# A one layer hybrid trunk on one core: the masked pairs written by VectorE, the norm sums and spreads asked for later

## The chip, the core and the metric

The kernel runs on one core of one Trainium2 chip. The metric is the device time of one execution in microseconds, the median of several runs. The engines are called PE (TensorE, matrix products and transposes), DVE (VectorE), ACT (ScalarE), POOL (GpSimd) and SP (SyncE, which issues DMAs here); PSUM banks take the results of PE.

## What is computed

One decoder layer on 2048 tokens of width 1024, all in float32: an RMSNorm with a shift and a scale from a conditioning vector, one combined input projection, three kinds of causal token mixers side by side, a per-head norm, a swish gate and an output projection; then a second norm, a gated feed-forward part with a causal convolution of width 3, and a last norm. Chunks have 64 tokens.

```python
def reference(x, c, w_in, ...):
    for l in range(DEPTH):                                   # DEPTH = 1
        mod = (c_act @ w_ada[l] + b_ada[l])[:, None, :]
        sh1, sc1, g1, sh2, sc2, g2 = jnp.split(mod, 6, axis=-1)
        h = rms_norm(x) * (1.0 + sc1) + sh1
        x = x + g1 * token_mixer(h, ...)                     # retention | HGRN2 | GLA, one in- and one out-projection
        h = rms_norm(x) * (1.0 + sc2) + sh2
        x = x + g2 * conv_ffn(h, ...)
    return rms_norm(x) * final_gain

# HGRN2 (8 heads, dk 64) and GLA (4 heads, dk 32): per-channel decay, one step per chunk
    cum = jnp.cumsum(gn, axis=2)
    rel = jnp.where(causal, cum[:, :, :, None, :] - cum[:, :, None, :, :], -jnp.inf)
    attn = jnp.einsum('bhid,bhjd,bhijd->bhij', qn, kn, jnp.exp(rel))
    o = jnp.einsum('bhij,bhje->bhie', attn, vn) + jnp.einsum('bhid,bhde->bhie', qn * jnp.exp(cum), s)
```

Retention (4 heads) has a fixed decay for each head instead. The attention inside a chunk, `attn`, is what the moved instruction begins to write.

## The kernel before

**Blocks and units.** The tokens are cut into four blocks of 512. In each block seven mixer units run in the order h0, h1, g, h2, h3, r0, r1: an h unit holds two HGRN2 heads, the g unit all GLA heads in two halves ("subs"), an r unit two retention heads. Tile names carry that letter (`ath`, `atg`, `qbg`, `kg`). The feed-forward part runs afterwards in two super-blocks of 1024 tokens. Almost every product is three matmuls (lines L254 to L256, operands split in a high and a low part), 128x512 or 128x256 each.

**Attention in a chunk** is `gated()`. The products of q and k on the diagonal, and of neighbours in a pair, are made by DVE, turned by four transposes each (L639), and summed (L643) into `dot`. One instruction (L649) multiplies them, broadcast, by a mask of pairs and so writes the whole 128x1024 tile `ath` or `atg`: the diagonal, the first level, and zeros elsewhere. Six levels follow (2, 4, ... 64 tokens): PE makes the level's products (L662, tile `lvh` or `lvg`), DVE decays q and k for the next level (L670, L672) and copies the level's quarter into the tile (L681, predicated; the widest ones are copied by ACT at L678). A later level waits for the decays of the one before. Then come the turned keys (L687), the state's update (`u` L701, `S` L711) and the outputs (L594, L596). There are 24 multiplies of L649: four units of h and two halves of g in each of four blocks.

**Norms.** The sum of squares of a block over its columns is gathered in an accumulator (`san` for the first and second norm, `n3a` for the last): a load of x on SP's queue, a square on ACT (L358), an add on DVE (L359), eight times. `rstd()` then has two parts: `first()` turns the accumulator by four transposes (`ssn`, L337), sums it on DVE and makes the reciprocal root by Newton steps (L155, L158 to L160, `rsn`); `second()`, `gap` later, spreads it over the partitions by four transposes (`bcn`, L348) and a copy on ACT. The same Newton lines serve the per-head norms of the mixers (`omsh`, `orsh`).

**What sets the order.** PE's order is written by hand through a clock of estimated time, `Clock`: every product advances it, and `clock.at(us, fn)` puts `fn` on the list at `us` from now. It is called when its time is reached while the main stream of projections is being written, so a larger number puts an operation further down PE's queue. `gated()` is a generator in such a list; its `yield PAIR_GAP` and `yield LEVEL_GAP` are the estimated time until its next operations. The other engines' order comes from a scheduler with priorities (`tc.high_priority(offset=CHAIN)` brings the chain of a unit forward), so it shifts with PE's. All engines work off their queue in order.

**Other work around it.** `sgg` (L561) are DVE's adds of the gate projection's parts; they free PSUM banks which the next projection, `pshfh`, needs. `es` (L1093 to L1096) are DVE's edge operations on tiles loaded from a scratch buffer in DRAM (`h2d`), for the feed-forward part; `wsd` (L945 to L948) are the same kind for weights. L316 and L247 split weights for the three matmuls. L365 and the `n2` jobs use the spreads.

Of the kernel before, what the change touches and what calls it, by code (L numbers as in the profile page):

```python
# [23 lines left out]
NB = SEQ // TB  # L24
# [26 lines left out]
CHAIN = 400  # L51

M512, M256, MF = 0.227, 0.12, 0.224
LEVEL_GAP, PAIR_GAP = (3.2, 4.8), 4.4
POST_GAP, LAST_GAP = 16.0, 12.0
JOB_RATE = 1.8

# [47 lines left out]
def trunk(ctx, tc, xT, vecs, cvec, cst, rope, msk, wada, win, walow, wgla, wout, wup, wdown, out):  # L105
# [13 lines left out]
    clock = Clock()  # L119
# [13 lines left out]
    def tmp(name, shape=(P, 512)):  # L133
        return pt.tile(list(shape), F32, tag="te", name=name, bufs=NTE)
# [4 lines left out]
    def small(name, n=8):  # L139
        return pc.tile([P, n], F32, tag="sm", name=name, bufs=8)  # L140

    V, S, G, T = nc.vector, nc.scalar, nc.gpsimd, nc.tensor
# [10 lines left out]
    def newton(x, y, n):  # L153

        V.tensor_scalar(y[:].bitcast(I32), x[:].bitcast(I32), -0.5, MAGIC, op0=ALU.mult, op1=ALU.add)  # L155
        a = small("nw", n)
        for _ in range(3):
            V.scalar_tensor_tensor(a[:], y[:], -0.5, y[:], op0=ALU.mult, op1=ALU.mult)  # L158
            V.tensor_tensor(a[:], a[:], x[:], op=ALU.mult)  # L159
            V.scalar_tensor_tensor(y[:], a[:], 1.5, y[:], op0=ALU.add, op1=ALU.mult)  # L160
# [97 lines left out]
    h = [None] * KD  # L258
# [71 lines left out]
    def rstd(acc, name, bc, then, bank=None, gap=4.5):  # L330

        bank = bank or late_ps

        def first():
            p = bank("ss" + name)
            for c in range(NCH):
                T.transpose(p[:, c * P:(c + 1) * P], acc[:, c * P:(c + 1) * P], ident)  # L337
            x, r = small("ms" + name, NCH), small("rs" + name, NCH)
            with tc.high_priority(offset=CHAIN):
                V.tensor_reduce(x[:], p[:].rearrange("p (c d) -> p c d", c=NCH), axis=mybir.AxisListType.X, op=ALU.add)  # L340
                V.tensor_scalar(x[:], x[:], 1.0 / D, EPS, op0=ALU.mult, op1=ALU.add)
                newton(x, r, NCH)
            clock.at(gap, lambda: second(r))

        def second(r):
            p = bank("bc" + name)
            for c in range(NCH):
                T.transpose(p[:, c * P:(c + 1) * P], r[:, c:c + 1].to_broadcast([P, P]), ident)  # L348
            S.copy(bc, p[:])
            then()  # L350
        return first

    def sumsq(acc, x, k, name, sl=slice(0, TB), first=None):
        if k == 0 if first is None else first:
            S.activation(acc[:, sl], x[:, sl], AF.Square)
        else:
            sq = late(f"sq{name}{k}")
            S.activation(sq[:, sl], x[:, sl], AF.Square)  # L358
            V.tensor_tensor(acc[:, sl], acc[:, sl], sq[:, sl], op=ALU.add)  # L359

    def new_acc(name):
        return px.tile([P, TB], F32, tag="ssacc", name="sa" + name, bufs=1)
# [12 lines left out]
    bc1 = {}  # L375
    done = set()
# [9 lines left out]
    def new_bc1(b):  # L386
        return px.tile([P, TB], F32, tag="bc1", name=f"bc1_{b}", bufs=1)
# [111 lines left out]
    def norm1_stat(b):  # L499
        acc = []  # L500

        def load(k):
            if not acc:
                acc.append(new_acc(f"n1_{b}"))
            x = tmp(f"x{b}_{k}")
            nc.sync.dma_start(x[:], xT[b, :, k, :])
            return x

        def add(x, k):
            sumsq(acc[0], x, k, f"n1_{b}_")  # L510
            if k == KD - 1:
                bc1[b] = new_bc1(b)
                clock.at(5.0, rstd(acc[0], f"n1_{b}", bc1[b][:], lambda: done.add(("n1", b)), gap=8.0))
        for k in range(KD):
            jobs.append((0.7, lambda k=k: load(k), lambda x, k=k: add(x, k)))

# [112 lines left out]
    def gated(name, b, ui, pos, kq, decay, subs, xy):  # L629
# [11 lines left out]
        with tc.high_priority(offset=CHAIN):  # L641
            for t, ps in enumerate(pss):
                V.tensor_reduce(dots[:, :, t], ps[:].rearrange("p (a d) -> p a d", a=NCH * nh),  # L643
                                axis=mybir.AxisListType.X, op=ALU.add)
            for i, _ in enumerate(subs):
                at = pa.tile([P, 8 * P], F32, tag="a4k", name=f"at{name}_{i}")
                d8 = dots[:].rearrange("p (a i) t -> p a i t", i=len(subs))[:, :, i, :]
                mk = m_all[:, M_PAIR:M_PAIR + P].bitcast(F32).rearrange("p (n t) -> p n t", t=2)
                G.tensor_tensor(at[:].rearrange("p (a n t) -> p a n t", a=8, t=2),  # L649
                                d8.unsqueeze(2).to_broadcast([P, 8, 64, 2]),  # L650
                                mk.unsqueeze(1).to_broadcast([P, 8, 64, 2]), op=ALU.mult)
                attns.append(at)
# [82 lines left out]
    def unit_h(b, u, pos, between=None):  # L735
# [19 lines left out]
        decay = decays(f, e)  # L755
        subs = [(q, rows, *tok_tiles(nm))]
        clock.chain(gated(nm, b, u, pos, kq, decay, subs, xy), 9.0 if b == u == 0 else 6.0)
        if b == 0 and u < 2:
            tok_evac(subs[0][2:], tf_gemm("vg" + nm, 4 * u + 2))
# [211 lines left out]
    def out_half(b, half, acc=None, after_pieces=None, begun=None):  # L971
        ops = [oTs[b][4 * half + k] for k in range(4)]
        for i in range(4):
            wp = begun[0] if begun and i == 0 else out_piece(b, half, i)
            if i == 3 and after_pieces:
                after_pieces()
            for m in (2 * i, 2 * i + 1):
                if half == 0:
                    x1[m] = x_tile(f"x1_{b}_{m}", m)
                    nc.sync.dma_start(x1[m], xT[b, :, m, :])  # L980
                early = begun and m < 2
                ps = begun[1][m] if early else acc_ps(f"y{b}_{half}_{m}")
                for k in range(3 if early else 0, 4):
                    out_step(ps, wp, m, k, ops[k])
                with tc.high_priority(offset=HOT):
                    V.scalar_tensor_tensor(x1[m], ps[:], G1[:, m:m + 1], x1[m], op0=ALU.mult, op1=ALU.add)
                if half == 1:
                    with tc.high_priority(offset=HOT):
                        sumsq(acc, x1[m], m, f"n2_{b}_")

    def out_finish(b, after_pieces=None, begun=None):


        acc = new_acc(f"n2_{b}")
        out_half(b, 1, acc, after_pieces, begun)
        rows = list(x1)
        bc = px.tile([P, TB], F32, tag="bc2", name=f"bc2_{b}", bufs=1)
        for m in range(KD if b == 0 else 0):
            nc.sync.dma_start(x1d[b, m][:], rows[m])

        def row_load(m):
            if b:
                nc.sync.dma_start(x1d[b, m][:], rows[m])
                return rows[m], rows[m] if b == NB - 1 else tmp(f"t2_{b}_{m}")[:]
            t = tmp(f"t2_{b}_{m}")[:]
            nc.sync.dma_start(t, x1d[b, m][:])
            return t, t

        def row(xt, m):
            x, t = xt  # L1010
            V.scalar_tensor_tensor(t, x, SC2[:, m:m + 1], bc[:], op0=ALU.mult, op1=ALU.mult)
            S.activation(t, t, AF.Identity, bias=SH2[:, m:m + 1])
            nc.sync.dma_start(h2d[b, m][:], t)
            if m == KD - 1:
                done.add(("n2", b))

        def then():
            if b == NB - 1:
                with tc.high_priority(offset=-100):
                    for m in range(KD):  # L1020
                        row(row_load(m), m)
                return
            for m in range(KD):
                jobs.append((0.75, lambda m=m: row_load(m), lambda xt, m=m: row(xt, m)))
        clock.at(5.0, rstd(acc, f"n2_{b}", bc[:], then, gap=8.0 if b < NB - 1 else 6.5))


    nth = {"w4": 0}
# [358 lines left out]
    def down_norm(s, h, y, acc, bc, bank=None):  # L1387
        b = 2 * s + h

        def then(m=0):  # L1390
            V.scalar_tensor_tensor(y[h, m], y[h, m], vec[:, V_FG + m:V_FG + m + 1], bc[:], op0=ALU.mult, op1=ALU.mult)
            nc.gpsimd.dma_start(out[b, :, m, :], y[h, m])
            if m == KD - 1:
                done.add(("n3", b))
            else:
                clock.at(1.4, lambda: then(m + 1))
        clock.at(7.0 if h else 12.0, rstd(acc, f"n3_{b}", bc[:], then, bank=bank, gap=4.5 if h else 9.0))

    def last_operands(s):

# [123 lines left out]
    with tc.high_priority(offset=100):  # L1524
        out_finish(NB - 1, lambda: up_weights(0, 0, A), out_begun)
# [121 lines left out]
```

## Time and profile before

| | |
|---|---|
| three runs | 2551.42, 2554.10, 2555.17 us; median 2554.1 |
| profiled execution | 2555.2 us; span from the first to the last instruction 2553.4 |
| mean granted TensorE clock | 0.989 |
| instructions | 35188 |
| POOL, L649 | 24 instructions, 49.5 us |

The span is that of the single profiled execution. Busy shares say how long an engine had work in flight, the list of waits what ended an engine's idle time, and the timeline when. PEclk in a window is the clock that was granted to PE: 1.00 is full speed.

### The profile page before, as it was taken

Reading aid. Unit: us, or ns where it says so; the run is one execution under the profiler, and the core shown is the slowest. Engines: PE = TensorE matmul, PEld = TensorE weight load, DVE = VectorE, ACT = ScalarE, POOL = GpSimd, SP = SyncE. Lnnn points to the kernel's source line nnn. Section 1 sums busy time; section 2 is a strip of 40 time slices with the busy share of each in tenths; the row PEclk is TensorE's granted clock in tenths of the full one; section 3 lists DMA queues with packets and bytes.
Section 4 is the critical chain, followed back from the end, with each engine's and each line's share of the span. In section 5 each row is a group of like instructions: output and inputs, shape, how many; then the busy total and the mean of one; then the engine's idle time right before and its main releaser. Section 6 shows DMA issues by size and latency. Waiting matters only on the chain.

```text
span 2553.4 us, 35188 instructions
## 1 busy us (share of the span) xinstructions
PE 2458.0 (96%) x12165; PEld 2061.8 (81%) x12165; DVE 2003.5 (78%) x3628; ACT 1148.0 (45%) x1950; POOL 195.8 (8%) x302
## 2 busy tenths in 40 slices
PE   5989999999999999999899999999989999999998
PEld 4878877778888888888778888888878888888887
DVE  8987877868779786886788888887688778778666
ACT  3333434334353344434455545555445455455542
POOL 1100000000000000000100000000001001000000
PEclk9999999999999999999999999999999999999999
DMA  8844549864588757896645445477675544447763
GB/s 312 295 140 132 173 142 326 291 219 154 198 268 303 250 170 230 278 314 217 197 164 184 153 145 165 145 263 250 209 233 174 154 147 145 149 141 248 224 191 132
DMA packets 232499, 525.12 MB, mean 206 GB/s; under 512 B 24928, under 2 KB 28032, under 8 KB 232320
## 3 DMA queue, kind: packets, MB, share of 16 engines
q1 hardware_dynamic: 229120, 512.38, 60.8%
q0 software_dynamic: 3200, 10.49, 1.2%
q8 instruction: 96, 1.57, 0.2%
q14 instruction: 83, 0.68, 0.1%
HBM read 397.46 MB, written 125.30 MB: 205 GB/s over the span
## 4 chain that ended last, share of the span: by engine, by line
PE 71%; DVE 13%; DMA 8%; issue 3%; ACT 2%; SPq 0%; DVEq 0%; POOL 0%; ACTq 0%; POOLq 0%
PE X L256 6%; PE X L254 6%; PE X L255 6%; PE Z L256 3%; PE Z L255 3%; PE Z L254 3%; PE dX L256 3%; PE dX L255 3%; PE dX L254 3%; PE lvh L662 2%; PE psqkvgr L254 2%; PE psqkvgr L256 2%; PE psqkvgr L255 2%; PE dY L256 2%; PE dY L255 2%
## 5 line engine op out<-in xcount | busy, mean ns | idle before, releaser
L254 PE MATMUL X<-B,A 128*128 128x512 f32 x572 | 223.6, 391 | 1.4 <-ACT u L1354 1.4
L256 PE MATMUL X<-B,A 128*128 128x512 f32 x572 | 223.1, 390 | 0.0
L255 PE MATMUL X<-B,A 128*128 128x512 f32 x572 | 223.0, 390 | 0.0
L1055 DVE TENSOR_TENSOR dA<-rd,dA 128x512 fp32r<-128x512 f32 x154 | 105.9, 689 | 86.6 <-ACT dA L1054 86.3
L1054 ACT CAST dA<-rd 128x512 fp32r<-128x512 f32 x154 | 95.5, 621 | 138.7 <-PE dY L256 42.7
L1055 DVE TENSOR_TENSOR A<-s,A 128x512 fp32r<-128x512 f32 x176 | 120.6, 686 | 36.1 <-ACT A L1054 35.8
L1054 ACT CAST A<-s 128x512 fp32r<-128x512 f32 x176 | 108.6, 618 | 71.4 <-PE Z L256 43.5
L254 PE MATMUL dX<-dB,dA 128*128 128x512 f32 x352 | 136.9, 389 | 0.0
L255 PE MATMUL dX<-dB,dA 128*128 128x512 f32 x352 | 136.9, 389 | 0.0
L256 PE MATMUL dX<-dB,dA 128*128 128x512 f32 x352 | 136.9, 389 | 0.0
L254 PEld LDWEIGHTS X<-B,A 128*128 128x128 f32 x572 | 107.7, 188 | 24.4 <-ACT u L1354 2.4
L256 PEld LDWEIGHTS X<-B,A 128*128 128x128 f32 x572 | 107.6, 188 | 22.4
L255 PEld LDWEIGHTS X<-B,A 128*128 128x128 f32 x572 | 107.7, 188 | 22.3
L255 PE MATMUL Z<-B,A 128*128 128x512 f32 x308 | 120.2, 390 | 2.8 <-DVE B L1055 2.8
L256 PE MATMUL Z<-B,A 128*128 128x512 f32 x308 | 120.1, 390 | 0.0
L254 PE MATMUL Z<-B,A 128*128 128x512 f32 x308 | 119.8, 389 | 0.0
L662 PEld LDWEIGHTS lvh<-qbh,kh 128*128 128x128 f32 x768 | 100.6, 193 | 22.0 <-issue 13.1
L662 PE MATMUL lvh<-qbh,kh 128*128 128x128 f32 x768 | 104.5, 279 | 10.2 <-DVE kh L672 8.8
L1055 DVE TENSOR_TENSOR dB<-rb,dB 128x512 fp32r<-128x512 f32 x154 | 105.5, 686 | 10.9 <-ACT dB L1054 10.7
L1055 DVE TENSOR_TENSOR A<-r,A 128x512 fp32r<-128x512 f32 x130 | 89.3, 687 | 27.3 <-ACT A L1054 27.2
L1054 ACT CAST A<-r 128x512 fp32r<-128x512 f32 x130 | 81.0, 623 | 63.8 <-PE Z L256 58.9
L254 PE MATMUL psqkvgr<-hqkvgr,ha 128*128 128x512 f32 x256 | 106.0, 414 | 0.4 <-DVE nw L159 0.2
(475 smaller groups left out, 7043.0 us busy)
## 6 DMA issues: line engine op xcount, KB each, us to landing
gs<-yv SPq DMA_DIRECT2D x154, 256.0 KB, 2.9
rb<-gs SPq DMA_DIRECT2D x154, 256.0 KB, 4.2
r<-wup SPq DMA_DIRECT2D x140, 256.0 KB, 3.5
s<-sumsu SPq DMA_DIRECT2D x136, 256.0 KB, 3.1
wada<-wada SPq DMA_DIRECT2D x48, 512.0 KB, 6.2
rd<-sumsd SPq DMA_DIRECT2D x88, 256.0 KB, 4.0
rd<-wdown SPq DMA_DIRECT2D x66, 256.0 KB, 3.9
x<-xT SPq DMA_DIRECT2D x64, 256.0 KB, 6.2
```

The lines of the kernel that those rows point to most:

```text
L254: T.matmul(ps, lhs[0], rhs[0], start=first, stop=False, skip_group_check=more)
L255: T.matmul(ps, lhs[0], rhs[1], start=False, stop=False, skip_group_check=more)
L256: T.matmul(ps, lhs[1], rhs[0], start=False, stop=last, skip_group_check=more)
L662: T.matmul(ps[:, c * P:(c + 1) * P].rearrange("p (h n s) -> p h n s", h=2, s=s), kq[:, c * P:(c + 1) * P], rhs, start=True, stop=True)
L1054: S.copy(hi, src)
L1055: V.tensor_tensor(lo, src, hi, op=ALU.subtract)
```

## The change

L649 goes from GpSimd (`G`) to VectorE (`V`). The estimated time between the transposes of the dots and the first level, `PAIR_GAP`, goes from 4.4 to 4.0. The sum of the first norm is asked for 14.0 instead of 5.0 after its last add was written, and its spread 9.5 instead of 8.0 after the sum. The gap of the second norm becomes 9.5 in all blocks, that of the last norm 10.0 in the first super-block and 8.0 in the second.

```diff
-LEVEL_GAP, PAIR_GAP = (3.2, 4.8), 4.4
+LEVEL_GAP, PAIR_GAP = (3.2, 4.8), 4.0
...
 # norm1_stat
-                clock.at(5.0, rstd(acc[0], f"n1_{b}", bc1[b][:], lambda: done.add(("n1", b)), gap=8.0))
+                clock.at(14.0, rstd(acc[0], f"n1_{b}", bc1[b][:], lambda: done.add(("n1", b)), gap=9.5))
...
 # gated
-                G.tensor_tensor(at[:].rearrange("p (a n t) -> p a n t", a=8, t=2),
+                V.tensor_tensor(at[:].rearrange("p (a n t) -> p a n t", a=8, t=2),
                                 d8.unsqueeze(2).to_broadcast([P, 8, 64, 2]),
                                 mk.unsqueeze(1).to_broadcast([P, 8, 64, 2]), op=ALU.mult)
...
 # out_finish
-        clock.at(5.0, rstd(acc, f"n2_{b}", bc[:], then, gap=8.0 if b < NB - 1 else 6.5))
+        clock.at(5.0, rstd(acc, f"n2_{b}", bc[:], then, gap=9.5))
...
 # down_norm
-        clock.at(7.0 if h else 12.0, rstd(acc, f"n3_{b}", bc[:], then, bank=bank, gap=4.5 if h else 9.0))
+        clock.at(7.0 if h else 12.0, rstd(acc, f"n3_{b}", bc[:], then, bank=bank, gap=8.0 if h else 10.0))
```

The order shows what moves. In the rows a tile's name ends in the numbers of its block or part and of its allocation; `x4` are four instructions of one form. First PE in block 0, where block 1's sum `ssn_1` is asked for among the value and gate products of h3. Before:

```order
L254 MATMUL psvgh_3_2_1780<-hvgh_3_0_1784,ha_0_440 128x512
L255 MATMUL psvgh_3_2_1780<-lvgh_3_0_1785,ha_0_440 128x512
L256 MATMUL psvgh_3_2_1780<-hvgh_3_0_1784,ha_0_440 128x512
L337 MATMUL ssn_1_1824<-c_all,san_1_1442 128x128 x4
L254 MATMUL psvgh_3_2_1780<-hvgh_3_0_1784,ha_1_455 128x512
```

Now the same products run on, and the sum stands at:

```order
L254 MATMUL psvgh_3_3_1796<-hvgh_3_1_1850,ha_3_529 128x512
L255 MATMUL psvgh_3_3_1796<-lvgh_3_1_1851,ha_3_529 128x512
L256 MATMUL psvgh_3_3_1796<-hvgh_3_1_1850,ha_3_529 128x512
L662 MATMUL lvg_32_1880<-qbg_0_1156,kg_989 128x128 x4
L662 MATMUL lvg_32_1885<-qbg_1_1165,kg_989 128x128 x4
L337 MATMUL ssn_1_1897<-c_all,san_1_1450 128x128 x4
L254 MATMUL psvgh_3_0_1793<-hvgh_3_2_1919,ha_4_557 128x512
```

Between the two places lie 33 products, the two halves of level 16 and those of level 32. On DVE the last add of that sum stands ahead of the decays for level 32, now with these rows between:

```order
L359 TENSOR_TENSOR san_1_1450<-san_1_1450,sqn_1_7_1805 128x512
L611 TENSOR_TENSOR xh_3_1774<-sqh_3_1771,kh_3_1628 128x512
L613 TENSOR_TENSOR kh_3_1628<-kh_3_1628,fh_3_1629 128x256
L614 TENSOR_TENSOR yh_3_1775<-sqh_3_1771,kh_3_1628 128x512
L615 TENSOR_TENSOR fh_3_1629<-fh_3_1629 128x256
L316 TENSOR_TENSOR lvgh_3_3_1967<-rvgh_3_3_1964,hvgh_3_3_1966 128x1024
L670 TENSOR_TENSOR qbg_0_1156<-qbg_0_1156,eg_991 128x32x16
```

Second, PE in block 1, around block 2's sum. Before it stood between two products of h3:

```order
L256 MATMUL psvgh_3_3_4592<-hvgh_3_1_4655,ha_2_2673 128x512
L337 MATMUL ssn_2_4693<-c_all,san_2_4451 128x128 x4
L254 MATMUL psvgh_3_3_4592<-hvgh_3_1_4655,ha_3_2679 128x512
L255 MATMUL psvgh_3_3_4592<-lvgh_3_1_4656,ha_3_2679 128x512
L256 MATMUL psvgh_3_3_4592<-hvgh_3_1_4655,ha_3_2679 128x512
```

Now it comes 28 rows later, behind the state products `ug`, 18 products of h3 and the outputs `og` of one half:

```order
L594 MATMUL og_0_4741<-S_111,qbg_0_3999 128x128
L596 MATMUL og_0_4741<-vg_0_4006,atg_0_4238 128x64 x2
L254 MATMUL psvgh_3_2_4591<-hvgh_3_2_4724,ha_4_2693 128x512
L255 MATMUL psvgh_3_2_4591<-lvgh_3_2_4725,ha_4_2693 128x512
L256 MATMUL psvgh_3_2_4591<-hvgh_3_2_4724,ha_4_2693 128x512
L337 MATMUL ssn_2_4777<-c_all,san_2_4451 128x128 x4
L254 MATMUL psvgh_3_2_4591<-hvgh_3_2_4724,ha_5_2699 128x512
```

Third, DVE in the g unit of block 3. Before, the gate adds L561 were mixed with the Newton steps of h1's norm, right behind the dots:

```order
L643 TENSOR_REDUCE dotg_9733<-dtg_1_9735 128x16
L570 TENSOR_SCALAR omsh_1_0_9716<-omsh_1_0_9716 128x8
L1096 TENSOR_TENSOR es_1_10270<-es_1_10270 128x512
L155 TENSOR_SCALAR orsh_1_0_9719<-omsh_1_0_9716 128x8
L561 TENSOR_TENSOR sgg_0_9536<-sgg_0_9536,psvgg_0_9546 128x128
L158 SCALAR_TENSOR_TENSOR nw<-orsh_1_0_9719 128x8
L561 TENSOR_TENSOR sgg_0_9536<-sgg_0_9536,psvgg_1_9547 128x128
```

Now the two multiplies, the first level's decays and its predicated copies are mixed with the Newton steps there. The rows from the second multiply on:

```order
L649 TENSOR_TENSOR atg_1_9739<-dotg_9724,m_all 128x1024
L159 TENSOR_TENSOR nw<-nw,omsh_1_0_9707 128x8
L670 TENSOR_TENSOR qbg_0_9528<-qbg_0_9528,fg_9302 128x256x2
L160 SCALAR_TENSOR_TENSOR orsh_1_0_9710<-nw,orsh_1_0_9710 128x8
L681 COPY_PREDICATED atg_0_9737<-m_all,lvg_2_9765 128x256x2
L158 SCALAR_TENSOR_TENSOR nw<-orsh_1_0_9710 128x8
L670 TENSOR_TENSOR qbg_1_9537<-qbg_1_9537,fg_9302 128x256x2
L159 TENSOR_TENSOR nw<-nw,omsh_1_0_9707 128x8
L672 TENSOR_TENSOR kg_9301<-kg_9301,fg_9302 128x128x2
L160 SCALAR_TENSOR_TENSOR orsh_1_0_9710<-nw,orsh_1_0_9710 128x8
L681 COPY_PREDICATED atg_1_9739<-m_all,lvg_2_9770 128x256x2
```

The first of the eight gate adds is the second row behind these, and behind the adds stand six operations on `es` (L1096, L1093 to L1096, L1093) ahead of the decays for the second level.

Elsewhere: in blocks 1 and 2 the gate adds of the g unit follow right behind its second multiply, earlier than before. The spread of the first norm's block 3 moves with its sum (30 rows later); that of the second norm's last block moves behind 12 more products, those of the last norm behind 3 to 15 more. The second norm's sums do not move. The loads of x for the sums stand at almost the same places of SP's queue; in block 1 the seventh now is ahead of a weight load and the last ahead of the pair of `wsd` loads.

## Prediction

> **What bounds the kernel now.** I read the shares of the page first, then the chain of work that ended last, TensorE's waits, the timeline of those waits, and windows around them.
>
> ```profile
> PE 2458.0 (96%) x12165; PEld 2061.8 (81%) x12165; DVE 2003.5 (78%) x3628; ACT 1148.0 (45%) x1950; POOL 195.8 (8%) x302
> ...
> PE 71%; DVE 13%; DMA 8%; issue 3%; ACT 2%; SPq 0%; DVEq 0%; POOL 0%; ACTq 0%; POOLq 0%
> ```
>
> TensorE is busy for 96% of the span and the diff leaves its matmuls as they are, so the time can only come from its gaps and from stretches at a lower clock. Windows of the two large stages (columns: length, then busy time of PE, PEld, DVE, ACT and POOL with instruction counts, granted clock, DMA share, GB/s) say which stage has gaps.
>
> ```profile
> 60.00:1262.00 1202.00, 1160.16 (x6374) 988.02 (x6373) 950.11 (x2137) 480.81 (x913) 97.09 (x118) 0.99 0.67 226
> 1300.00:1885.00 585.00, 584.32 (x2580) 483.44 (x2579) 473.51 (x635) 302.18 (x471) 30.52 (x82) 1.00 0.58 190
> ```
>
> The mixers (first row) leave PE idle for 1202.0 - 1160.2 = 41.8 us; the first feed-forward half (second row) for 0.7 us, with 584.32 / 2580 = 0.226 us for a matmul there. So all that matters lies in the mixers and at the norms. The waits of PE (us in total, times, longest) name the producers, and the timeline places them; the bracket of a row is the idle time ahead of it.
>
> ```profile
> PE ssn L337 <- DVE san L359: 17.2, 3, 11.4
> PE ssn L431 <- DVE san L359: 14.2, 1, 14.2
> PE lvh L662 <- DVE kh L672: 8.8, 9, 3.8
> PE bcn L348 <- DVE rsn L160: 7.1, 3, 2.9
> ...
> PE pshfh L254 <- DVE nw L158: 2.4, 1, 2.4
> ...
> PE pshfh L254 <- DVE nw L159: 1.3, 2, 0.7
> ```
> ```profile
> 182.87 1.12 PE L337 MATMUL ssn<-c_all,san 128*128 128x128 f32 x4 [5.62 <-DVE san L359]
> ...
> 349.97 0.55 PE L662 MATMUL lvh<-qbh,kh 128*128 128x128 f32 x1 [3.78 <-DVE kh L672]
> ...
> 516.65 1.11 PE L337 MATMUL ssn<-c_all,san 128*128 128x128 f32 x4 [11.38 <-DVE san L359]
> ...
> 817.29 0.62 PE L348 MATMUL bcn<-c_all,rsn 128*128 128x128 f32 x4 [1.45 <-DVE rsn L160]
> ...
> 1067.57 0.47 PE L254 MATMUL pshfh<-ha,hhfh 128*128 128x512 f32 x1 [2.35 <-DVE nw L158]
> ...
> 1285.00 0.62 PE L348 MATMUL bcn<-c_all,rsn 128*128 128x128 f32 x4 [2.88 <-DVE rsn L160]
> ...
> 1892.35 0.65 PE L348 MATMUL bcn<-c_all,rsn 128*128 128x128 f32 x4 [2.77 <-DVE rsn L160]
> ```
>
> The 14.2 us at L431 is the start of the program and stays. A long wait is paid twice, since the clock halves behind it:
>
> ```profile
> 181.10:187.90 6.80, 5.03 (x14) 4.17 (x15) 6.08 (x21) 0.04 (x1) 0.00 (x0) 0.50 0.01 2
> 348.30:358.60 10.30, 7.42 (x27) 6.61 (x28) 9.28 (x19) 0.69 (x1) 0.00 (x0) 0.50 0.34 103
> 508.80:522.40 13.60, 5.75 (x21) 5.17 (x22) 6.84 (x20) 2.30 (x3) 0.00 (x0) 0.50 0.82 280
> 1068.60:1072.00 3.40, 3.40 (x10) 2.63 (x9) 3.40 (x9) 1.42 (x4) 0.00 (x0) 0.51 0.28 67
> ```
>
> PE work done at 0.50 takes twice its full-speed time, so half of the busy time in a row is the price: 2.5 us behind the 5.62 wait, 2.9 behind the 11.38, 1.7 even behind the 2.35.
>
> **The norm sums and spreads, asked for later.**
>
> *Block 1's sum (the wait at 182.87).* Its place moves behind 33 products and two level sets.
>
> ```profile
> 182.13 0.69 DVE L359 TENSOR_TENSOR san<-san,sqn 128x512 f32<-128x512 f32 x1
> 182.73 0.68 DVE L611 TENSOR_TENSOR xh<-sqh,kh 128x512 f32<-128x512 f32 x1
> ...
> 190.52 1.95 PE L662 MATMUL lvg<-qbg,kg 128*128 128x128 f32 x16
> ```
>
> That is 33 x 0.226 + 2 x 1.8 (a set of 16 records lasts 1.95 with its overlapping tail) = 11 us, counted from 182.87 - 5.62 = 177.25: PE comes to 188, the last add ends at 182.8. The whole wait and its half clock go: 5.62 + 2.5 = 8.1. What is late next is the level behind it. The decays that release the set of level 32 stand on VectorE behind that last add, after four operations of the next pair of heads, a weight split and then three decays. With 0.6 to 0.7 for a 512 column operation, 0.4 for 256 columns and 1.2 for 1024, that is about 5.2 us, so 187.9; PE, with no sum to wait for, is there at 186.5. I give back 1.4 for it and 0.5 for level 16 in the same way: 6.2 (bounds 3.0, if VectorE is behind by another 3 us, and 8.1).
>
> *Block 2's sum (516.65).* It moves behind 28 rows of PE: 18 products (4.1 us), 16 records of u (1.5) and one head group's outputs (2.6), so 8.2. The sum is late because its inputs are:
>
> ```profile
> 511.13 0.63 ACT L358 ACTIVATE sqn<-x 128x512 f32<-128x512 f32 x1 [5.01 <-DMA x<-xT]
> 515.24 0.63 ACT L358 ACTIVATE sqn<-x 128x512 f32<-128x512 f32 x1 [3.48 <-DVE wsd L946]
> ...
> 515.90 0.69 DVE L359 TENSOR_TENSOR san<-san,sqn 128x512 f32<-128x512 f32 x1
> ```
>
> The last two loads of x landed 4 us apart, and each square waited for its load. The order of loads in SP's queue changes little there: the seventh load now stands ahead of a weight load, the last ahead of a pair of scratch loads, so they come no later. The wait falls from 11.38 to 3.2 or less. Behind 2.35 the trace has one stretch of half clock worth 1.7, so I keep that. Gain 8.2 + 2.9 - 1.7 = 9.4; bounds 0 (the loads come later as PE runs on) and 11.38 + 2.9 = 14.3.
>
> [...]
>
> *Spreads.* 817.29: the gap from sum to spread grows from 8.0 to 9.5, more than the wait of 1.45, which goes: 1.45. 1285.00 (second norm of the last block, 6.5 to 9.5): the spread moves behind 12 products, 12 x 0.226 = 2.7 of the 2.88. 1892.35: only 3 products are put between, 0.7 of 2.77. The other spreads and the second-norm sums had no wait. Together 4.85; bounds 1.5 and 7.1 (all three waits).
>
> Norm part: 6.2 + 9.4 + 4.85 = 20.4.
>
> **The multiply on VectorE.** 24 instructions leave GpSimd, two of them in each GLA unit and one in each of 16 others, and VectorE takes them.
>
> ```profile
> L649 POOL TENSOR_TENSOR ath<-doth,m_all 128x1024 f32<-128x1024 f32 x16 | 33.1, 2070 | 114.6 <-DVE doth L643 98.7 <-DVE omsg L570 8.1 <-DVE omsh L570 5.8
> L649 POOL TENSOR_TENSOR atg<-dotg,m_all 128x1024 f32<-128x1024 f32 x8 | 16.4, 2077 | 7.3 <-DVE omsh L570 4.0 <-DVE dotg L643 3.3
> ...
> L1312 DVE TENSOR_TENSOR yv<-yv,yg 128x1024 f32<-128x1024 f32 x44 | 53.8, 1223 | 1.0
> ```
>
> The nearest row for the new price is L1312, a product of two 128x1024 tiles on VectorE: 1.22 each, 24 x 1.22 = 29.3 us. But VectorE pays already while GpSimd multiplies:
>
> ```profile
> 342.00 2.08 DVE L754 TENSOR_TENSOR qbh<-sqh,fh 64x512 f32<-64x512 f32 x1
> 344.20 0.69 DVE L754 TENSOR_TENSOR qbh<-sqh,fh 64x512 f32<-64x512 f32 x1
> ...
> 348.72 0.69 DVE L670 TENSOR_TENSOR qbh<-qbh,fh 128x512 f32<-128x512 f32 x1
> ...
> 456.68 3.79 POOL L649 TENSOR_TENSOR atg<-dotg,m_all 128x1024 f32<-128x1024 f32 x2 [1.09 <-DVE dotg L643]
> ...
> 457.16 1.47 DVE L570 TENSOR_SCALAR omsh<-omsh 128x8 f32<-128x8 f32 x1
> 458.66 1.84 DVE L155 TENSOR_SCALAR orsh<-omsh 128x8 int32<-128x8 int32 x1
> ...
> L155 DVE TENSOR_SCALAR orsh<-omsh 128x8 int32<-128x8 int32 x16 | 11.2, 700 | 0.3
> ...
> L155 DVE TENSOR_SCALAR orsr<-omsr 128x8 int32<-128x8 int32 x8 | 1.4, 172 | 0.3
> ```
>
> The two tiny instructions end with the two multiplies and take 1.47 and 1.84 where the same form beside no GpSimd work takes 0.17: 2.97 for two multiplies, 1.5 for one, 24 x 1.5 = 36 us. (The group of 16 alone has 16 x (0.700 - 0.172) = 8.4 of it.) So VectorE's own time goes by 29.3 - 36 = -7 us, bounds +21 (if only the 8.4 is freed) and -7. It is hidden or not by where it stands, which I take place by place.
>
> Gains: in blocks 1 and 2 the adds that free the banks of pshfh come ahead of the level work, and the two waits on L159 go: 1.3. In the first pair of block 1 (the wait of 3.78 at 349.97) the qb product at 342.00 lasts 2.08 where the multiply holds it and its twin at 344.20 takes 0.69, so 1.4 comes back; from that twin to the decay at 348.72 the trace has 4.5 us, and the new order puts there its 0.7, the multiply (1.22), a weight split (1.22), and some small operations (0.8), 3.9 in all. I take 2 off that wait, and 1 off the other 5.0 us of level waits, most of them in block 0: 3. Bounds 0 and 3.78 + 7.42 / 2 + 5.0 = 12.5.
>
> Losses, in block 3's GLA unit:
>
> ```profile
> 1067.14 0.28 DVE L561 TENSOR_TENSOR sgg<-sgg,psvgg 128x128 f32<-128x128 f32 x1
> ...
> 1075.91 0.69 DVE L1093 TENSOR_TENSOR es<-es 128x512 f32<-128x512 f32 x1 [1.60 <-DMA es<-h2d]
> ```
>
> The third gate add (1067.14) frees the bank for which PE waited at 1067.57. It now stands behind both multiplies (2.4) and the first level's two q decays, one k decay and two predicated copies (4.2), instead of behind the two stretched instructions (3.3): 3.3 later, with a little clock -3.5. The edge work (L1093 to L1096) stands with five more operations ahead of the second level's decays and waited for a load before; its load is asked for earlier, so -2.5, between 0 and -6. The reordering of priorities moves small waits of 0.3 to 1.0 both ways in 24 units: -2, as an estimate from the nine waits of level products that have 8.8 in all; bounds -9 and +5.
>
> Multiply part: 1.3 + 3 - 3.5 - 2.5 - 2 = -3.7. GpSimd's own end is not on the path: its share of the chain is 0%.
>
> **Sum.** 20.4 - 3.7 = 16.7 off the profiled execution of 2555.2: 2538.5. The median of the runs, 2554.1, is 1.1 lower: 2537.4, so 2537.
>
> **Rivals.**
>
> A, the wait at block 2's sum moves with the work. For it: the loads of x wait for buffers and share SP with weights, and the last square's releaser was L946, work that itself follows PE. Against it: the loads' place in SP comes forward. Then 9.4 becomes 0: 2537 + 9.4 = 2546.5.
>
> B, slower: VectorE is the bound of the level chain. Each multiply is now in front of the first level's decays of its unit on the one engine that makes them, where it ran beside them. For it: DVE is 9.28 busy of 10.30 in the window at 348, 6.08 of 6.80 at 181. If a share s of 29.3 comes to PE and nothing of the 36 is returned there, the loss is 29.3 s; it outweighs the norm part's 20.4 from s = 0.7, and at s = 1 the time is 2554 - 20.4 + 29.3 = 2563. Against it: in the rows at 457 and 458 VectorE stands still as long, before the same decays.
>
> C, block 3's GLA unit becomes the new wait: the edge work waits in front of the decays for its loads, PE for level 2 and for the gate adds, at half clock. At 6 more than in my sum plus a window of 1.7, 2537 + 8 = 2545.
>
> D, more is returned: the residual at 516 vanishes (14.3 for 9.4) and the 346 chain goes whole (7.5 for 2): 2537 - 10.4 = 2527.
>
> E, the delay does not do what it says: the last add fixes sum and spread alike, and the spread, now 9.5 behind a sum that is itself later, becomes what the next block's normalization waits for. Then the 6.2 and 9.4 come back there: 2537 + 15.6 = 2552.6. Against it: in the trace only the three spreads listed waited, and none of their readers shows in the table of PE's waits.
>
> **How the numbers follow.** My forecast has 0.42, A 0.15, B 0.11, C 0.12, D 0.15, E 0.05. Its own range is 2532 to 2543. The range that holds 8 in 10 leaves out B with most of E above and the tail of D below: 2524 to 2550. A measurement of this kernel can tell about 0.2%, 5.1 us: faster is below 2549. The forecast, A, C and D are on that side but for a margin of A and C (0.05), so faster 0.79; within 0.2% E, that margin and a part of B, 0.12; slower the rest of B, 0.09.
>
> **What would show it.** Right: no wait on L337 over 4 us, no half clock at 182, and bcn of L348 with under 3 us in all; 24 DVE rows of L649 near 1.22, L155 at 0.17 everywhere, DVE's busy sum near 1996. Wrong: L649 on DVE over 1.5, lvh and lvg of L662 waiting over 20 us in all where 8.8 stood, or ssn L337 of block 2 still above 8.

## The result

The changed kernel took 2533.0 us (median of 4 runs, 2529.94 to 2536.13) beside 2552.8 for the kernel before on the same chip: ratio 0.9923, 95% interval 0.9906 to 0.9940. A second comparison gave 0.9930 (0.9917 to 0.9942). That is 18 to 20 us faster, where 2537 was forecast. The total is right. Its two parts, the experiments show, are not: the norms' later places are worth 3 to 5 us and not 20, and the multiply with the shorter `PAIR_GAP` is worth 13 to 15 and not -4. (Differences in us are taken from the ratios.)

The profile after has the same matmuls in a shorter span (2531.4). DVE has the 24 instructions and yet less busy time, and the chain that ended last has more of PE and less of DVE and DMA:

```profile
PE 2452.0 (97%) x12165; PEld 2059.3 (81%) x12165; DVE 1989.5 (79%) x3652; ACT 1147.5 (45%) x1950; POOL 146.3 (6%) x278
...
PE 82%; DVE 8%; DMA 5%; issue 2%; ACT 1%; SPq 0%; DVEq 0%; POOL 0%; ACTq 0%; POOLq 0%
```

Of DVE's groups (mean in ns behind the busy time), the moved multiply, and the tiny Newton instruction that had 700 ns before:

```profile
L649 DVE TENSOR_TENSOR ath<-doth,m_all 128x1024 f32<-128x1024 f32 x16 | 19.5, 1218 | 0.0
L649 DVE TENSOR_TENSOR atg<-dotg,m_all 128x1024 f32<-128x1024 f32 x8 | 9.7, 1218 | 0.0
L155 DVE TENSOR_SCALAR orsh<-omsh 128x8 int32<-128x8 int32 x16 | 2.7, 168 | 0.2
```

Both prices of the forecast hold: 1.218 for 1.22, 0.168 for 0.17. DVE's sum fell by 14.0, with 29.2 added, so 43.2 us or 1.8 for each multiply were freed (forecast 36 and 1.5; the fall of 14.0 is beyond the bound of 7). The waits of PE, first the table, then those of its rows that stand at the places of the forecast:

```profile
PE ssn L431 <- DVE san L359: 14.6, 1, 14.6
PE lvh L662 <- DVE kh L672: 7.1, 6, 3.8
PE X L254 <- ACT A L1054: 6.2, 2, 5.1
PE pshfh L254 <- DVE sgg L561: 4.5, 1, 4.5
```
```profile
177.10 0.80 PE L254 MATMUL psvgh<-hvgh,ha 128*128 128x512 f32 x1 [3.66 <-DVE sqh L749]
...
343.47 2.05 PE L662 MATMUL lvh<-qbh,kh 128*128 128x128 f32 x8 [3.77 <-DVE kh L672]
...
1045.55 0.76 PE L254 MATMUL pshfh<-ha,hhfh 128*128 128x512 f32 x1 [4.45 <-DVE sgg L561]
...
1867.25 0.32 PE L348 MATMUL bcn<-c_all,rsn 128*128 128x128 f32 x1 [2.02 <-DVE rsn L160]
...
1886.00 0.63 PE L254 MATMUL X<-hB,A 128*128 128x512 f32 x1 [5.11 <-ACT A L1054]
```

The waits of 5.6 and 11.4 for the sums of blocks 1 and 2 are gone. In place of the first PE now waits 3.66 for `sqh`, and the clock still halves there (176.1 to 183.0, before 181.1 to 187.9). Block 3's gate adds hold PE for 4.45; the last norm's spread waits 2.02 and a cast behind it 5.11, where before it stood at

```profile
1910.11 0.50 PE L254 MATMUL X<-hB,A 128*128 128x512 f32 x1 [2.62 <-ACT A L1054]
```

### The profile page after: what moved, and what is told of

Its sections match the earlier page's. It is cut to its first block, busy times and chain, and to the rows that moved or that the text cites. A ratio compares the mean times of both kernels' runs of the same rounds, so it can differ in the third digit from the quotient of the medians.

```text
span 2531.4 us, 35178 instructions
## 1 busy us (share of the span) xinstructions
PE 2452.0 (97%) x12165; PEld 2059.3 (81%) x12165; DVE 1989.5 (79%) x3652; ACT 1147.5 (45%) x1950; POOL 146.3 (6%) x278
## 4 chain that ended last, share of the span: by engine, by line
PE 82%; DVE 8%; DMA 5%; issue 2%; ACT 1%; SPq 0%; DVEq 0%; POOL 0%; ACTq 0%; POOLq 0%
PE X L254 6%; PE X L256 6%; PE X L255 6%; PE Z L256 3%; PE Z L255 3%; PE Z L254 3%; PE lvh L662 3%; PE dX L256 3%; PE dX L255 3%; PE dX L254 3%; PE psqkvgr L254 2%; PE psqkvgr L256 2%; PE psqkvgr L255 2%; PE y L254 2%; PE y L256 2%
## 5 line engine op out<-in xcount | busy, mean ns | idle before, releaser
L254 PE MATMUL X<-B,A 128*128 128x512 f32 x572 | 224.4, 392 | 1.4 <-ACT u L1354 1.4
L256 PE MATMUL X<-B,A 128*128 128x512 f32 x572 | 223.6, 391 | 0.0
L254 PE MATMUL dX<-dB,dA 128*128 128x512 f32 x352 | 136.9, 389 | 0.0
L256 PE MATMUL dX<-dB,dA 128*128 128x512 f32 x352 | 136.9, 389 | 0.0
L254 PEld LDWEIGHTS X<-B,A 128*128 128x128 f32 x572 | 108.2, 189 | 24.5 <-ACT u L1354 2.2
L256 PEld LDWEIGHTS X<-B,A 128*128 128x128 f32 x572 | 108.2, 189 | 22.7
L254 PE MATMUL Z<-B,A 128*128 128x512 f32 x308 | 119.9, 389 | 0.0
L256 PE MATMUL Z<-B,A 128*128 128x512 f32 x308 | 119.8, 389 | 0.0
L254 PE MATMUL psqkvgr<-hqkvgr,ha 128*128 128x512 f32 x256 | 106.1, 415 | 1.1 <-DVE orsg L160 1.0
```

What stands on the lines that cost most here:

```text
L254: T.matmul(ps, lhs[0], rhs[0], start=first, stop=False, skip_group_check=more)
L256: T.matmul(ps, lhs[1], rhs[0], start=False, stop=last, skip_group_check=more)
```

## Experiments

The change has three parts: the multiply on VectorE, `PAIR_GAP` 4.0, and the norms' later places. All eight combinations were timed, each against the kernel before on its chip; other kernels take one suspect each.

**The multiply alone.**

```diff
-                G.tensor_tensor(at[:]...
+                V.tensor_tensor(at[:]...
```

> The change's VectorE multiply alone; PAIR_GAP and all the norms' places stay as before. Theory (the norms pay, the multiply about breaks even): the waits of L337 stay near 5.6 and 11.4 with their half clock, DVE's busy sum falls by 36 - 29 = 7 to 14 us, and the time is within 5 us of before (2548 to 2558). Rival (the blocking by GpSimd was what cost the time): 10 us or more faster, under 2543, with the waits of L662 and pshfh gone.

Measured: ratio 1.0025 (1.0013 to 1.0037), 2558.2 beside 2550.6: 6 us slower. The multiply alone is a small loss, as the forecast had it (3.7), and just outside the expected range.

**The norms alone.**

```diff
-                clock.at(5.0, rstd(acc[0], f"n1_{b}", ..., gap=8.0))
+                clock.at(14.0, rstd(acc[0], f"n1_{b}", ..., gap=9.5))
... (and the gaps of the second and the last norm, as in the change)
```

> The later sums and spreads alone; the multiply stays on GpSimd with PAIR_GAP 4.4. Theory: the waits of 5.6 and 11.4 go from L337 and the time falls by 15 to 24 us, to 2529 to 2538, as much as the whole change. Rival (the sums' waits only move unless VectorE is also freed from GpSimd's blocking): under 10 us faster, over 2543, with new waits of 3 us and more behind the old places.

Measured: 0.9982 (0.9972 to 0.9991), 2547.4: 4 us faster, the rival's number. Its trace shows where block 2's gain went. The timeline at that sum, DVE and then PE:

```profile
510.11 0.69 DVE L359 TENSOR_TENSOR san<-san,sqn 128x512 f32<-128x512 f32 x1 [4.11 <-ACT sqn L358]
510.72 0.26 DVE L711 SCALAR_TENSOR_TENSOR S<-S,eg,ug 32x64 f32<-32x64 f32 x1
...
514.53 0.55 PE L594 MATMUL og<-S,qbg 128*128 128x128 f32 x1 [3.73 <-DVE S L711]
```

The last add but one waits for its late square, idling DVE for 4.1 us, and the state updates `S` of the g unit stand behind it in DVE's queue. PE no longer waits for the sum; it waits for the state, 3.73 us, in front of the outputs. Three stretches of half clock follow this wait, and two more stand in block 1 behind waits of 0.85 and 1.97 for `pshfh`, which the kernel before has too (0.84 and 1.99) at full clock:

```profile
513.10:523.34 10.24, 8.81 (x35) 8.26 (x36) 7.18 (x22) 1.84 (x3) 1.04 (x2) 0.50 0.71 237
...
311.70:318.50 6.80, 5.94 (x14) 4.72 (x15) 3.98 (x10) 2.03 (x3) 0.00 (x0) 0.50 0.40 153
```

At half of PE's busy time, an estimate (128x512 products of L254 to L256 start 0.43 us apart at half clock in the kernel before and 0.23 at full), they cost 4.4 and 3.0 us; at block 2's sum that was 2.9 before. In the changed kernel the two instructions of DVE:

```profile
496.22 0.69 DVE L359 TENSOR_TENSOR san<-san,sqn 128x512 f32<-128x512 f32 x1 [0.81 <-ACT sqn L358]
497.91 0.27 DVE L711 SCALAR_TENSOR_TENSOR S<-S,eg,ug 32x64 f32<-32x64 f32 x1 [1.00 <-PE ug L701]
```

Here `S` waits for PE and not for a load: the add was early enough.

**GpSimd's multiply done twice**, in the kernel before.

```diff
+                for _ in range(2):
-                G.tensor_tensor(at[:]...
+                    G.tensor_tensor(at[:]...
```

> The kernel before with GpSimd's multiply L649 done twice into the same tile, so that GpSimd multiplies for 3.8 us in place of 1.9 in each of 24 places; nothing else changes. Blocking theory: VectorE loses another 1.0 to 1.9 us in each place, DVE's busy sum rises by 25 to 45 us with the same instructions, and the time by 5 to 25 us. Rival (VectorE's stretched instructions wait for data or for something else, not for GpSimd): DVE's sum stays within 5 us of 2003.5, and the time within 5 us, since the tile is needed first by L681 some microseconds later.

Measured: 1.0147 (1.0127 to 1.0166), 2589.3: 38 us slower, more than was expected. Groups of DVE and the page's engine row:

```profile
PE 2466.6 (95%) x12165; PEld 2067.4 (80%) x12165; DVE 2039.9 (79%) x3628; ACT 1148.1 (44%) x1950; POOL 245.2 (9%) x326
...
L570 DVE TENSOR_SCALAR omsh<-omsh 128x8 f32<-128x8 f32 x16 | 14.3, 896 | 0.1
L155 DVE TENSOR_SCALAR orsh<-omsh 128x8 int32<-128x8 int32 x16 | 14.1, 880 | 0.3
```

With the same 3628 instructions DVE's sum is 36.4 us higher, 1.5 for each added multiply. So GpSimd's multiply takes time from VectorE here. The other candidate, the tile that is finished later, hardly shows: in this trace one weight load waits for the multiply, once, for 2.5 us, and no instruction of DVE does; PE's added waits are nearly all for DVE. Of the 1.9 us that one multiply takes on GpSimd (median of L649's 16 on `ath` in the kernel before, 1.907), VectorE lost 1.5 by this trace and gets 1.8 back by the change.

**The rest of the eight.**

> The multiply on VectorE and PAIR_GAP 4.0; the norms' places as before. Theory I (the sums' delay is needed, and the freed VectorE makes it pay): near the multiply alone, 2553 to 2560 beside 2550.6 of before, with the waits of L337 near 6 and 10. Theory II (PAIR_GAP is what turns the multiply's loss into a gain): 2538 to 2547.

```diff
 # on the kernel before
-LEVEL_GAP, PAIR_GAP = (3.2, 4.8), 4.4
+LEVEL_GAP, PAIR_GAP = (3.2, 4.8), 4.0
-                G.tensor_tensor(at[:]...
+                V.tensor_tensor(at[:]...
```

> The multiply on VectorE and all the norms' later places, with PAIR_GAP 4.4 as before. Theory I: within 4 us of the whole change, 2529 to 2537, and no wait of PE for S or san behind 500. Theory II: the parts add up without PAIR_GAP, -4 (norms alone) + 6 (multiply alone), so 2550 to 2556.

```diff
 # on the changed kernel
-LEVEL_GAP, PAIR_GAP = (3.2, 4.8), 4.0
+LEVEL_GAP, PAIR_GAP = (3.2, 4.8), 4.4
```

> PAIR_GAP 4.0 and all the norms' later places, with the multiply on GpSimd. Theory I: as the norms alone, 2543 to 2551, with PE waiting for S behind a late add of san near 510. Theory II: 2530 to 2540.

```diff
 # on the changed kernel
-                V.tensor_tensor(at[:]...
+                G.tensor_tensor(at[:]...
```

> The whole change once more, on the same chip and with the same runs of before as the three beside it: 17 to 22 us faster than before, if it is the reference that the others are held against.

(no edit to the changed kernel)

> PAIR_GAP 4.0 alone; the multiply on GpSimd, the norms as before. Theory J (the shorter gap pays only with the multiply on VectorE, the tile being written earlier and nothing blocked): within 4 us of before. Theory K (the gap alone moves the places that matter, and the multiply adds little): 10 to 16 us faster, as the multiply and the gap together were.

```diff
 # on the kernel before
-LEVEL_GAP, PAIR_GAP = (3.2, 4.8), 4.4
+LEVEL_GAP, PAIR_GAP = (3.2, 4.8), 4.0
```

All of them, as ratios to the kernel before with their intervals:

| multiply on | PAIR_GAP | norms as before | norms later |
|---|---|---|---|
| GpSimd | 4.4 | 1 | 0.9982 (0.9972 to 0.9991) |
| VectorE | 4.4 | 1.0025 (1.0013 to 1.0037) | 1.0034 (1.0021 to 1.0046) |
| GpSimd | 4.0 | 1.0032 (1.0020 to 1.0044) | 0.9977 (0.9966 to 0.9987) |
| VectorE | 4.0 | 0.9943 (0.9930 to 0.9955) | 0.9930 (0.9917 to 0.9942) |

`PAIR_GAP` turns the multiply's loss into a gain, and it does so only with the multiply on VectorE. No theory's ranges hold throughout. Of theory II the first range does (2538.0); the multiply and the norms at 4.4 are slower than both theories had it (2562.5); for `PAIR_GAP` and the norms theory I's range holds (2549.7), with PE's wait for `S` at 511. `PAIR_GAP` alone excludes theory K, but it is 8 us slower and not within theory J's 4. What the two give together beyond their sum is 0.9943 - 1.0025 - 1.0032 + 1 = -0.0114, some 29 us, with the norms as before, and 0.9930 - 1.0034 - 0.9977 + 0.9982 = -0.0099, 25 us, with the norms later; the intervals of the ratios leave each uncertain by about 6 us. The norms' places are worth +0.1% to -0.6%, depending on what stands beside them, and -0.13% on top of the other two, where the intervals overlap.

Where in the program the parts pay can be read from the start of the k-th projection product on PE in each trace, counted from 0, in us against the kernel before (its own time in brackets; V is the multiply on VectorE). These are single executions: two of the changed kernel differ by up to 3.6 here. For `PAIR_GAP` alone the profiled one is the fastest of its six, for both the slowest of its five.

| product | V | PAIR_GAP | both | norms | V, norms | PAIR_GAP, norms | all |
|---|---|---|---|---|---|---|---|
| 600th (203) | -1.9 | -1.6 | -4.4 | -3.4 | -5.0 | -2.2 | -4.8 |
| 1050th (370) | -2.0 | -6.1 | -11.3 | -1.3 | -3.7 | -4.8 | -11.3 |
| 1350th (464) | -2.1 | -5.8 | -11.0 | -0.8 | -3.0 | -4.0 | -9.8 |
| 1650th (578) | +0.3 | -3.7 | -16.6 | -6.7 | -8.8 | -8.1 | -23.8 |
| 2850th (966) | -0.1 | -0.9 | -15.7 | -3.7 | -0.8 | -3.9 | -25.4 |
| 3600th (1208) | +6.0 | +5.2 | -10.0 | -5.0 | +6.0 | -4.3 | -19.2 |
| 4200th (1371) | +5.2 | -0.5 | -13.1 | -8.4 | +2.4 | -11.1 | -25.1 |
| last (2540) | +4.0 | -2.7 | -13.0 | -6.4 | +7.3 | -9.7 | -22.0 |

The joint gain, both minus each alone, is 3 us by the 1350th product, 13 by the 1650th and 14 at the end with the norms as before; with the norms later it is 4, 14 and 26. What the two have in common falls between the 1350th and the 1650th product.

The stretch from the 600th to the 1050th, with the first pair of block 1, is mostly `PAIR_GAP`'s own. In the kernel before, PE waits there 0.43, 3.78 and 1.21 in a row. The multiply alone changes that to:

```profile
343.65 1.15 PE L662 MATMUL lvh<-qbh,kh 128*128 128x128 f32 x8 [0.22 <-DVE qbh L754]
...
347.79 1.13 PE L662 MATMUL lvh<-qbh,kh 128*128 128x128 f32 x8 [3.00 <-DVE nw L158]
...
351.33 2.05 PE L662 MATMUL lvh<-qbh,kh 128*128 128x128 f32 x8 [2.41 <-DVE kh L672]
```

With both, one wait of 3.77 is left (as in the changed kernel at 343.47 above), and one stretch of half clock where before there were three. With `PAIR_GAP` alone it is one wait and one stretch as well, and 4.5 of the 6.9 us that both gain there:

```profile
348.76 2.04 PE L662 MATMUL lvh<-qbh,kh 128*128 128x128 f32 x8 [4.28 <-DVE kh L672]
```

Between the 1350th and the 1650th lies block 2's sum, in which the loads of x matter: the last add but one starts 42 to 43 us behind PE's 1350th product with both parts (with or without the norms), and 45 to 48 behind it in the other six traces. With the norms later another 11 us of the joint gain fall between the 1650th and the 2850th: the multiply and the norms at 4.4 have there a wait for the gate adds, with three stretches of half clock behind it, that the changed kernel has not:

```profile
767.56 0.77 PE L254 MATMUL pshfh<-ha,hhfh 128*128 128x512 f32 x1 [6.75 <-DVE sgg L561]
```

Which engine's order differs can be said. By line and tile name (without the allocation numbers) PE's 12165 matmuls start in the same order with the multiply on either engine, in each of the four pairs of the table; `PAIR_GAP` alone changes the name at 3283 of the places. It also moves the sum of block 1 by 11 rows, behind the products of level 16, without any delay in the norm. So on one order of PE the multiply on VectorE loses 0.25% or 0.52%, and on the other it gains 0.89% or 0.47%. Why DVE and the loads suit the second order and not the first is not settled.

**PAIR_GAP 4.2**, in the changed kernel.

```diff
-LEVEL_GAP, PAIR_GAP = (3.2, 4.8), 4.0
+LEVEL_GAP, PAIR_GAP = (3.2, 4.8), 4.2
```

> The whole change with PAIR_GAP 4.2, half way between 4.4 (9 us slower than before) and 4.0 (18 us faster). Theory J1 (a shorter gap steadily shortens each unit's chain): about half way, 4 to 9 us faster than before. Theory J2 (the gap acts through the order that comes out of it, in which whole operations change places): near one of the ends, or beside both.

Measured: 0.9978 (0.9969 to 0.9988), about half way between 1.0034 and 0.9930 (0.9982). This fits theory J1, a steady gain with a shorter gap. One point between two cannot exclude that the order happened to fall so.

**The last norm's gaps as before**, in the changed kernel.

```diff
-        clock.at(7.0 if h else 12.0, rstd(..., gap=8.0 if h else 10.0))
+        clock.at(7.0 if h else 12.0, rstd(..., gap=4.5 if h else 9.0))
```

> The changed kernel with the last norm's gaps as before (9.0 and 4.5). Theory A (from the changed kernel's trace, where PE waits 5.1 us for a cast of A at 1886 in place of 2.6 before): the longer gaps of the last norm cost about 4 us, so this is 4 us faster than the changed kernel, near 2529. Theory B (the term of my forecast): they gain 0.7 us, so near 2534. Theory C: no difference within 2 us, the 5.1 us wait being there in both.

Measured: 0.9916 (0.9900 to 0.9931), 2530.6. It is 2 us below the changed kernel's 2533.0, with intervals that overlap: not told apart by itself. In its trace the spread waits 4.4 and the cast behind it 1.2, against 2.0 and 5.1: what the later spread saves comes back one step on.

**The gate adds first.** L561 of the four-projection units gets a higher priority.

```diff
+            with tc.high_priority(offset=HOT):
-            V.tensor_tensor(sg[:, c, :], sg[:, c, :], gate, op=ALU.mult)
+                V.tensor_tensor(sg[:, c, :], sg[:, c, :], gate, op=ALU.mult)
```

> The whole change, with the gate adds L561 of the units with four projections given the higher priority HOT on DVE, so that in block 3's g unit they no longer stand behind both multiplies and the first level. If those places cost what the forecast put on them (3.5 us, in the changed kernel's trace a wait of 4.5 at 1041 with two half clock stretches): 3 to 6 us faster than the whole change (20 to 24 faster than before), and that wait under 2. If the level chain, which now comes behind the adds, is late in their place: no difference within 2 us, and a wait of L662 near there.

Measured: 0.9936 (0.9918 to 0.9954), 2534.0: no gain. The wait at 1041 is gone, and between the 2850th and the 3600th product this kernel gains 2 us where the changed one loses 6. But at the 1650th it is 16 us ahead of before and the changed one 24; in block 1 the new order brings other waits:

```profile
498.47 3.47 PE L702 MATMUL ug<-vg,kTg 128*128 128x128 f32 x16 [2.35 <-ACT kTg L691]
...
520.89 0.29 PE L348 MATMUL bcn<-c_all,rsn 128*128 128x128 f32 x1 [2.70 <-DVE orsg L160]
```

So the place does cost about what was put on it, and the edit that mends it gains nothing in all, because the order changes at other places too.

**Both of these.**

> The same with the last norm's gaps as before (9.0 and 4.5). If both places pay on their own: 2 us faster than the one with the adds first, 22 to 27 faster than before. If the last norm's gaps are worth nothing: the same within 1 us.

Measured: 0.9915 (0.9902 to 0.9928), 2526.6, the lowest of all. It is below the changed kernel in its two comparisons (0.9923, 0.9930), with overlapping intervals, and level with the kernel in which only the last norm's gaps are as before. Of two kernels that differ only in these gaps the one with the shorter was ahead both times (0.9916 to 0.9923 and 0.9930, and 0.9915 to 0.9936): likely a small loss within the change, not a settled one.

## Why the prediction was right, and where not

- *DVE's prices.* Right: 1.22 for the multiply, and the stretched instructions back at 0.17. The freed time was 43 us, the forecast's 36 too low.
- *The signs.* No wait on L337 is over 2.64 and `bcn` of L348 has 2.0 in all, as forecast. But the half clock at 182 has not gone: it stands at 176 to 183, behind the wait for `sqh`.
- *Norm part, 20.4.* This is the term that was mis-sized: alone it gives 4.6 (0.18%), on top of the rest 3.3 (0.13%). For block 1's sum 6.2 was put down, and 3.4 is gained by the 600th product with the norms alone, inside the bounds; what is late next is `sqh` (3.66), not the set of level 32. `PAIR_GAP` takes that wait too: without any delay in the norms, PE's wait for sums is down to block 2's alone. For block 2's sum 9.4 was put down; from the 1350th to the 1650th product the norms alone gain 5.9. The wait that is left, 3.73, is near the 3.2 of the forecast, but it is another wait: one queue further, for what stands behind the late add on DVE, which the prediction did not ask for. What was mis-sized more is the clock behind it, 4.4 where 1.7 was kept. Besides, 2.6 of block 1's 3.4 are lost again by the 1350th product, where the two new stretches of half clock stand (3.0). By the 2850th 3.7 are left of the norms' gain.
- *Multiply part, -3.7.* Mis-sized the other way. The multiply alone measured -6, so its own terms were near in sum. But `PAIR_GAP` was given no term at all, and what it moves on PE was put at nothing without a reason. With it, the part is +14.6 (0.57%).
- *Block 3's g unit, -3.5 and -2.5.* Right in sum, in part by luck: from the 2850th to the 3600th product the changed kernel loses 6.2 of its lead (6.0 forecast). Of this the gate adds, for which PE waits 4.45 instead of 2.35, make 2.1 and some 0.5 of half clock. The edge work does wait for its load on DVE (3.95 at 1051), but PE does not wait for the second level behind it; other waits, 1.25 at 1002 and 1.00 at 1111, come in its place. And the multiply's place is not needed for the wait: all four traces with it on VectorE have 4.4 to 6.1 there, and of the four with it on GpSimd `PAIR_GAP` alone has it too, with a loss of 6.1:

```profile
1070.20 0.77 PE L254 MATMUL pshfh<-ha,hhfh 128*128 128x512 f32 x1 [6.26 <-DVE sgg L561]
```

- *Spreads, 4.85.* The waits of 1.45 and 2.88 are gone and 0.75 of 2.77 went as forecast, but behind the last one a wait of 2.62 grew to 5.11.
- *Rivals.* B in its strong form, VectorE outweighing the norms, came true for one combination that was not the change: multiply and norms at `PAIR_GAP` 4.4 are 0.34% slower. D came true at block 2 in the whole change: 14.0 are gained between the 1350th and the 1650th product, its 14.3. C's loss beyond the sum and E's waits for the spreads do not show. The fault in the working was that the parts were added as if they were independent; the interaction of two of them, 25 to 29 us, is larger than any term of the sum. That the total came out near 2533 is owed to two errors that cancel.

## What to carry to other kernels

When a change edits a schedule's constant next to an engine move, time all the combinations before giving either part the credit: here each alone was a loss and both together a gain of 15 us. When a wait for a late input is to be removed by asking for the result later, look at the queue of the engine that makes the input: here what stood behind the late instruction there, the state `S`, became the next wait (3.73 us). And a mend at one place that goes through a scheduler is a change of the whole order, so read the trace at the places that were good before.

## What was not expected of the hardware

The half clock behind a wait was not a fixed price. Two executions of the same changed kernel both have a wait of 2.64 us in front of block 3's sum; PE's clock is the column of 1.00 and 0.50 in these windows, each taken behind that wait. The first profile:

```profile
792.00:796.00 4.00, 3.94 (x23) 3.50 (x24) 3.78 (x13) 1.05 (x1) 0.00 (x0) 1.00 0.54 182
```

and the second execution:

```profile
788.90:792.30 3.40, 3.40 (x12) 2.72 (x11) 3.17 (x12) 1.05 (x1) 0.00 (x0) 0.50 0.64 212
```

So the same wait cost nothing in the first and 1.7 us (half of 3.40, an estimate) in the second. The wait of 3.66 at 173 has two stretches of 3.41 us at half clock with it in the first (176.14 to 182.97), and the wait of 2.35 in the kernel before has one (1068.55 to 1071.96).

The traces show where such stretches stand. In the kernel before they start at 181.09, 348.34, 508.77 and 1068.55, which are 49, 47 and 164 steps of 3.413 us apart; in the first profile of the changed kernel those at 176.14, 343.40 and 1043.13 are 49 and 205 such steps apart. The steps with the wait of 2.64, two of the first profile, over which it is spread, and one of the second execution, which holds the whole of it:

```profile
787.13:790.54 3.41, 2.29 (x19) 2.01 (x17) 1.78 (x7) 0.00 (x0) 0.00 (x0) 1.00 0.99 378
790.54:793.96 3.42, 1.91 (x11) 1.69 (x12) 3.10 (x11) 0.54 (x1) 0.00 (x0) 1.00 0.46 188
...
785.51:788.92 3.41, 0.77 (x8) 0.61 (x7) 3.06 (x12) 0.00 (x0) 0.00 (x0) 1.00 0.97 392
```

PE was busy for 2.29 and 1.91 us of the first two, and the clock stayed; for 0.77 of the third, and it halved. Divided into such steps between 100 and 2500 us, the traces of the kernel before and of the changed one have eleven at full clock with 1.38 us of busy PE or less, and half clock follows each; it follows none with 1.72 or more. Of the two between, it follows the one with 1.53 and not the one with 1.50.
